# Sparse attention's compressed-branch values: two F32R passes on split operands in place of plain F32

## The chip, the cores and the metric

The kernel runs on one NeuronCore of a Trainium2 chip. The metric is device microseconds of one execution. The engines are named as in the profile: PE is TensorE (matmuls; PEld are its weight loads), DVE VectorE, ACT ScalarE, POOL GpSimd, SP the engine that issues the DMAs. PSUM is used as banks of 128 partitions by 512 words.

## The reference, cut to what matters

Two decoder layers over 512 positions of width 1024. Layer 0 has a gating MLP, differential attention and memory attention; layer 1 has a convolution module, a sparse attention with 8 heads in 2 groups, and memory attention. The change concerns one of three branches of the sparse attention: keys and values are compressed to 31 blocks, every query attends to the blocks that end before it, and the output of this branch is added, weighted by a gate, to those of the two others.

```python
kc = compress(k_cmp_raw, ...)              # 31 compressed keys a group
vc = compress(v_cmp_raw, ...)              # 31 compressed values a group, 64 wide
def block(args):                           # 128 queries
    s = einsum('bgrqd,bgnd->bgrqn', qi, kc) * scale
    p_c = masked_softmax(s, cmp_end <= qpos)
    o_c = einsum('bgrqn,bgnd->bgrqd', p_c, vc)
    ...                                    # o_s (selected blocks), o_w (window)
    return gt[..., 0:1] * o_c + gt[..., 1:2] * o_s + gt[..., 2:3] * o_w
```

## The kernel before

**Dense products.** A matrix is split in a high part, rounded to F32R, and a low part, the rest. A product is three F32R matmuls (high by high, high by low, low by high: L402, L403, L404 in `mm3`). The split of a weight is ACT's copy L386 and POOL's subtraction L389; the split of something in PSUM or of an activation is `split`: ACT's copy L376 and DVE's subtraction L377. Transposes are L399.

**Sparse attention** is `d_attn`, over query tiles in the order 3, 2, 1, 0 and two groups of four heads in each. `d_cattn` does the compressed branch of a tile for all 8 heads: scores L1148, softmax on DVE and ACT, transposes, and a copy (L1167) to `pc`, the weights of 32 compressed positions x 4 heads on the partitions, 128 queries along the free dimension, one such square a group. `d_cmp` has earlier put the compressed values in `cbd`: for head r of a group a block of 32 rows holds the 64 value columns, the other rows are zero, so that one product over 128 partitions picks out head r. L1184 does this product, plain F32, once a head, into rows 0 to 63 of the group's bank `o`.

The two other branches are steps (a, b) in the same loop: scores in L927, from PSUM with the mask by DVE's L929, exponentials in ACT's L1191, reciprocals and gates L1192 and L1193, a scaling on DVE (L576) or POOL (L574) in turn, transposes L399, a split to `pe`, and value products L1214: high and low part of the values side by side (128 weight columns, rows 0 to 127 of `o`), and the high part alone for the low part of `pe` (64 columns). A tile of index i has i + 1 key tiles; tiles 3 and 2 work on two heads a step, tiles 1 and 0 on four. After a group ACT copies the upper half of `o` (L1219), DVE adds it to the lower (L1220) and the gate multiplies (L582). There are two PSUM banks for scores, two for transposes and one for `o`.

**What runs beside it.** `merge` puts dense work between the steps: gate projections (`gates_T`, with DVE's L479), the end of the convolution (`c_finish`: DVE's L1305, L1307, L1309), then the output projection `out_part`, whose sums DVE adds to the residual (L657). The order in which the engines execute is fixed when the program is built: a scheduler lists instructions by priority and by when their operands and buffers are expected free.

**Pages.** Working tiles are pages of an arena. F32R tiles lie in arena "r", in pages of 2048 words a partition (kinds x and w), which `take` halves when half a page is enough; F32 tiles lie in arena "f". A page that was given back is taken again, and what is written to it must wait for the last reader. `take` goes by the smallest size with a free page, and prefers a larger one only while more than `RESERVE` (2 for x and w) of that size are free:

```python
sizes = [size for k, size in sorted(self.free) if k == kd and size >= words and self.free[k, size]]
if sizes:
    pick = sizes[0]
    for size in sizes[1:]:
        if words > 16 and size <= 4 * words and len(self.free[kd, size]) > RESERVE[kd in "xw"] \
                and self.free[kd, size][0][0] < self.free[kd, pick][0][0]:
            pick = size
```

While `d_attn` runs on tiles 3 and 2, two pages of kind x are free for it. A `pe` takes 1024 words (two key tiles) or 512.

Of the kernel before, what the change touches and what calls it, by code (L numbers as in the profile page):

```python
# [24 lines left out]
F32R = mybir.dt.float32r  # L25
BF16 = mybir.dt.bfloat16
AF = mybir.ActivationFunctionType
ALU = mybir.AluOpType
AX = mybir.AxisListType
ADD, SUB, MUL, MAX = ALU.add, ALU.subtract, ALU.mult, ALU.max  # L30

P = 128
# [253 lines left out]
def emit(ctx, tc, nc, D, out):  # L286
    sbp = ctx.enter_context(tc.tile_pool(name="sb", bufs=1))
# [4 lines left out]
              "p": Arena(psp.tile([P, words["p"]], F32, name="banks"), PAGES["p"])}  # L292
    cst_t = sbp.tile([P, CONST], F32, name="const")

    def SC():
        return Scope(arenas)
# [8 lines left out]
    V, A, G, mm = nc.vector, nc.scalar, nc.gpsimd, nc.tensor.matmul  # L305
    dma = nc.sync.dma_start
    act = A.activation
# [4 lines left out]
    def bc(ap, shape):  # L312
        return ap.broadcast_to(list(shape))
# [24 lines left out]
    def C(shape):  # L338
        n = int(np.prod(shape[1:]))
        v = cst_t[:shape[0], coff[0]:coff[0] + n]  # L340
        coff[0] += n
        assert coff[0] <= CONST
        if len(shape) == 3:
            v = v.rearrange("p (a b) -> p a b", a=shape[1])
        elif len(shape) == 4:
            v = v.rearrange("p (a b c) -> p a b c", a=shape[1], b=shape[2])
        return v
# [11 lines left out]
    def colp(n):  # L359
        o, l = COFF[n]  # L360
        return col[:, o:o + l]
# [6 lines left out]
    def rstd(sc, ss, scale, n, eps=EPS, parts=P):  # L368
        v = sc([P, n])[:parts]
        G.tensor_scalar(v, ss, scale, eps, MUL, ADD)  # L370
        r = sc([P, n])[:parts]
        G.tensor_tensor(r, v, mhalf[:parts, :n], ALU.pow)  # L372
        return r

    def split(src, h, l, eng=None):
        act(h, src, AF.Copy)  # L376
        (eng or V).tensor_tensor(l, src, f32(h), SUB)  # L377
# [20 lines left out]
    def tr(o, i, k=P):  # L398
        nc.tensor.transpose(o, i, ident[:k, :k])  # L399
# [27 lines left out]
    def proj_T(sc, hs, name, kind="d"):  # L427
        p = sc.ps(kind, [P, S])
        with SC() as wsc:
            (wh, wl), = load(wsc, name)  # L430
            wh = wh.rearrange("p (k c) -> p k c", k=KT)
            wl = wl.rearrange("p (k c) -> p k c", k=KT)
            for k in range(KT):
                mm3(p, wh[:, k, :], wl[:, k, :], hs[0][k // 4][:, k % 4, :], hs[1][k // 4][:, k % 4, :],
                    k == 0, k == KT - 1)
        return p
# [621 lines left out]


    ckt = sbp.tile([P, 2, 64], F32R, name="ckt")  # L1060
    cbd = C([P, 2, 4, 64])
    ccm = sbp.tile([P, NT, 32], BF16, name="ccm")

    def d_cmp():
        w2 = C([P, 2, 64])
        dma(w2, D["w2"].rearrange("p (a d) -> p a d", a=2))
        for j, nm in enumerate(("kc", "vc")):
            sc = SC()
            f = sc([P, 2, S])
            with SC() as pc:  # L1070
                p = proj_T(pc, h1, nm, "t")
                for g in range(2):
                    act(f[0:64, g, :], p[64 * g:64 * g + 64, :], AF.Copy)
                    V.tensor_copy(f[64:128, g, 0:511], p[64 * g:64 * g + 64, 1:512])
            yield UT
            w1 = [sc([P, 8, P], F32, k) for k in ("f", "raw")]
            for b in range(2):
                dma(w1[b], D["w1"][j, :, b * DM:(b + 1) * DM].rearrange("p (l c) -> p l c", l=8))
            fe = sc([P, 16, 64])
            f4 = fe.rearrange("p l (g j) -> p l g j", g=2)  # L1080
            pos = colp("posk" if j == 0 else "posv")
            G.memset(f4[:, :, :, 31:32], 0.0)
            for g in range(2):
                for a in range(2):
                    G.tensor_tensor(f4[:, 8 * a:8 * a + 8, g, 0:31],
                                    f[:, g, 16 * a:16 * a + 496].rearrange("p (j l b) -> p l j b", l=8, b=2)[:, :, :, 0],
                                    bc(pos[:, 8 * a:8 * a + 8].unsqueeze(2), [P, 8, 31]), ADD)
            hp = sc.ps("t", [64, P])
            for l in range(16):
                mm(hp, fe[:, l, :], w1[l // 8][:, l % 8, :], start=l == 0, stop=l == 15)  # L1090
            ht, th = sc([64, P]), sc([P, 64])
            act(ht, hp, AF.Tanh, scale=0.5)
            V.scalar_tensor_tensor(ht, ht, 1.0, hp, ADD, MUL)
            with SC() as pc:
                pt = pc.ps("t", [P, 64])
                tr(pt, ht, 64)
                V.tensor_copy(th, pt)
            o = sc.ps("t", [64, 64])
            mm(o, th, w2[:, j, :], start=True, stop=True)
            if j == 0:  # L1100
                t, u, d = sc([64, 64]), sc([64, 16]), sc([64, 2, 64])
                ss = sc([64, 1])
                act(t, o, AF.Square, accum_out=ss)
                r = rstd(sc, ss, 0.25 / 64, 1, parts=64)
                G.tensor_scalar(r, r, 0.5, None, MUL)
                V.tensor_tensor(t, o, ccg, MUL)
                V.tensor_tensor(u, o[:, 0:16], csg, MUL)
                V.tensor_tensor(t[:, 0:8], t[:, 0:8], u[:, 8:16], ADD)
                V.tensor_tensor(t[:, 8:16], t[:, 8:16], u[:, 0:8], ADD)
                V.tensor_scalar(d, bc(t.unsqueeze(1), [64, 2, 64]), r, None, MUL)  # L1110
                pt = sc.ps("d", [P, 64])
                tr(pt, d.rearrange("p a d -> p (a d)"), 64)
                split(pt.rearrange("p (g j) -> p g j", g=2), ckt[:, :, 0:32], ckt[:, :, 32:64])
            else:
                G.memset(cbd, 0.0)
                for g in range(2):
                    for r in range(4):
                        act(cbd[32 * r:32 * r + 32, g, r, :], o[32 * g:32 * g + 32, :], AF.Copy, scale=0.5)
            sc.close()
            yield 3700  # L1120
        G.memset(ccm, 0.0)
        G.affine_select(ccm, ccm, pattern=[[P, NT], [-16, 32]], compare_op=ALU.is_ge, fill=NEG, base=-31,
                        channel_multiplier=1)
        G.affine_select(ccm, ccm, pattern=[[0, NT], [-1, 32]], compare_op=ALU.is_ge, fill=NEG, base=30,
                        channel_multiplier=0)
# [17 lines left out]
    def d_cattn(i, pc):  # L1143

        with SC() as sc:
            s2 = sc.ps("s", [P, 8, 64])
            for h in range(8):
                mm(s2[:, h, :], dqs[i][0][:, h, :], ckt[:, h // 4], start=h == 0, stop=False)  # L1148
            mm(s2[:, :, 0:32], identb, bc(ccm[:, i:i + 1, :], [P, 8, 32]), start=False, stop=True)
            s = sc([P, 8, 32])  # L1150
            act(s, s2[:, :, 32:64], AF.Copy)
            V.tensor_tensor(s, s, s2[:, :, 0:32], ADD)
            mx, lc = sc([P, 8]), sc([P, 8])
            V.tensor_reduce(mx, s, AX.X, MAX)
            V.tensor_scalar(mx, mx, 0.1 * NEG, None, MAX)
            sm = sc([P, 8, 32])
            V.tensor_tensor(sm, s, bc(mx.unsqueeze(2), [P, 8, 32]), SUB)
            act(sm, sm, AF.Exp)
            V.tensor_reduce(lc, sm, AX.X, ADD)
            V.tensor_scalar(lc, lc, tiny, None, MAX)  # L1160
            V.reciprocal(lc, lc)
            V.tensor_tensor(lc, lc, dgt[:, i, :, 0], MUL)
            V.tensor_tensor(sm, sm, bc(lc.unsqueeze(2), [P, 8, 32]), MUL)
            pt = sc.ps("t", [P, 2, P])
            for g in range(2):
                tr(pt[:, g, :], sm[:, 4 * g:4 * g + 4, :].rearrange("p h j -> p (h j)"))
            act(pc, pt, AF.Copy)  # L1167
        yield CX

    def d_attn(yD, order, done):  # L1170

        for i in order:
            isc = SC()
            pc = isc([P, 2, P])
            yield from d_cattn(i, pc)
            for g in range(2):
                gsc = SC()
                o = gsc.ps("o", [P, 4, P])
                nh = 4 if i < WIDE else 2
                steps = [(a, b) for a in range(0, 4, nh) for b in range(2)]  # L1180
                for a, b in steps:
                    if (a, b) == steps[-1]:
                        for r in range(4):
                            mm(o[0:64, r, :], cbd[:, g, r, :], pc[:, g, :], start=False, stop=False)  # L1184
                    with SC() as sc:
                        es, nm = causal_scores(sc, i, [[(dqs[i][0][:, 4 * g + r, :], dkh[:, 2 * b + g, :]),
                                                        (dqs[i][0][:, 4 * g + r, :], dkl[:, 2 * b + g, :])]
# [9 lines left out]
                        for k0 in range(0, i + 1, kn):  # L1197
                            ks = range(k0, min(k0 + kn, i + 1))
                            n = len(ks)
                            with SC() as pc2:  # L1200
                                pt = pc2.ps("t", [P, n, nh, P])
# [5 lines left out]
                                for k in ks:  # L1207
# [5 lines left out]
                                    for m in ((hi, lo) if b + k == 0 else (lo, hi)):  # L1213
                                        mm(*m, start=m is hi and a + b + k == 0,  # L1214
                                           stop=m is hi and (a, b) == steps[-1] and k == i)
# [142 lines left out]
         "r": {"x": [(2048, 7)], "w": [(2048, 5)]},  # L1358
         "p": {"d": [(512, 6)], "t": [(512, 2)]}}
RESERVE = [3, 2]  # L1360
CONST = 3370

W_DENSE, W_ATTN, W_OUT, W_ATTN1 = 5, 5, 4, 2
P_DENSE, P_L0, P_MEM = (5, 0, 3, 0), (3, 2, 2, 1), (4, 2, 2, 0)
# [31 lines left out]
```

## Time and profile before

| | us |
|---|---|
| timed runs | 708.21, 708.18, 705.78 |
| their median | 708.18 |
| the profiled execution | 705.86 |
| its span | 704.1 |
| mean granted clock of PE | 0.99 |

The span runs from the first to the last instruction; the 1.76 us between it and the execution's time lie around it. A stretch's table gives each engine's busy time and, in brackets, its instructions; busy PE counts matmuls that overlap once, and the duration of one matmul (some 0.4 us for 512 columns) is longer than the distance to the next (0.23).

### The profile page before, as it was taken

How to read it: one execution, taken by the hardware profiler on the slowest of the kernel's cores; microseconds unless marked ns; L12 is line 12 of the kernel's file. 1: busy time of each engine (PE TensorE's matmuls, PEld its weight loads, DVE VectorE, ACT ScalarE, POOL GpSimd, SP SyncE). 2: the span in 40 equal slices, each digit the busy share in tenths (PEclk: the TensorE clock that was granted, in tenths of full speed). 3: DMA queues.
4: the chain of work that ended last, by engine and by line, in shares of the span. 5: the costliest groups of instructions: out<-in, count | busy, mean ns of one | idle time of the engine just before them, and what ended most of it. 6: DMA issues, size and time to landing. Idle time of an engine off the chain costs nothing.

```text
span 704.1 us, 11050 instructions
## 1 busy us (share of the span) xinstructions
PE 667.0 (95%) x3819; PEld 564.9 (80%) x3819; DVE 496.6 (71%) x1204; ACT 376.8 (54%) x846; POOL 392.7 (56%) x414
## 2 busy tenths in 40 slices
PE   4999989999999979989989999898999999999997
PEld 3789989888888867878878888776777888788875
DVE  4606678667666975763474968998867776998773
ACT  6345346556455772762453568642346666676541
POOL 3467887575336763255854789965564523421650
PEclk9999999999999988999999999999999999999999
DMA  8532135564313352123332421104121101120121
GB/s 316 174 119 91 61 90 152 142 169 131 105 53 121 104 174 82 61 91 110 105 102 80 150 76 48 57 1 150 36 85 60 61 31 60 54 68 1 61 76 74
DMA packets 22376, 66.56 MB, mean 95 GB/s; under 512 B 3504, under 2 KB 3760, under 8 KB 22320
## 3 DMA queue, kind: packets, MB, share of 16 engines
q1 hardware_dynamic: 22320, 65.86, 28.7%
q8 instruction: 30, 0.49, 0.3%
q14 instruction: 26, 0.21, 0.1%
HBM read 57.46 MB, written 2.10 MB: 85 GB/s over the span
## 4 chain that ended last, share of the span: by engine, by line
PE 72%; DVE 12%; POOL 6%; ACT 4%; issue 3%; DMA 3%; SPq 0%; ACTq 0%; POOLq 0%; DVEq 0%
PE banks L403 18%; PE banks L402 18%; PE banks L404 18%; PE banks L399 6%; PE banks L927 4%; DVE arena_r L377 3%; POOL arena_r L389 3%; DMA arena_f<-in_wall_dram 2%; POOL arena_f L372 2%; PE banks L1214 2%; PE banks L965 2%; ACT arena_r L386 1%; DVE arena_f L929 1%; PE banks L1090 1%; PE banks L1184 1%
## 5 line engine op out<-in xcount | busy, mean ns | idle before, releaser
L389 POOL TENSOR_TENSOR arena_r<-arena_f,arena_r 128x512 fp32r<-128x512 f32 (+1 forms) x174 | 228.6, 1339 | 174.9 <-ACT arena_r L386 171.1
L402 PE MATMUL banks<-arena_r 128*128 128x512 f32 (+2 forms) x784 | 289.7, 374 | 5.6 <-ACT arena_r L386 2.3
L403 PE MATMUL banks<-arena_r 128*128 128x512 f32 (+2 forms) x784 | 290.3, 371 | 2.4 <-POOL arena_r L389 1.4
L404 PE MATMUL banks<-arena_r 128*128 128x512 f32 (+2 forms) x784 | 288.8, 370 | 1.5 <-DVE arena_r L377 1.5
L402 PEld LDWEIGHTS banks<-arena_r 128*128 128x128 f32 x784 | 148.6, 190 | 31.2 <-ACT arena_r L386 3.7
L403 PEld LDWEIGHTS banks<-arena_r 128*128 128x128 f32 x784 | 149.0, 190 | 26.1 <-POOL arena_r L389 2.9
L404 PEld LDWEIGHTS banks<-arena_r 128*128 128x128 f32 x784 | 148.8, 190 | 24.2 <-DVE arena_r L377 2.2
L386 ACT ACTIVATE arena_r<-arena_f 128x1024 fp32r<-128x1024 f32 (+2 forms) x87 | 91.1, 1049 | 74.2 <-DMA arena_f<-in_wall_dram 19.8
L399 PE MATMUL banks<-const,arena_f 128*128 128x128 f32 x507 | 83.4, 281 | 15.8 <-DVE arena_f L417 8.9
L377 DVE TENSOR_TENSOR arena_r<-banks,arena_r 128x512 fp32r<-128x512 f32 (+1 forms) x112 | 67.1, 608 | 27.6 <-ACT arena_r L376 27.1
L376 ACT ACTIVATE arena_r<-banks 128x512 fp32r<-128x512 f32 (+1 forms) x112 | 57.7, 532 | 51.6 <-PE banks L399 36.5
L399 PEld LDWEIGHTS banks<-const,arena_f 128*128 128x128 f32 x507 | 62.4, 145 | 28.3 <-DVE arena_f L417 9.3
L929 DVE CUSTOM_DVE_ANT_0 arena_f<-banks,const 128x512 f32<-128x512 f32 (+3 forms) x128 | 60.5, 485 | 32.4 <-PE banks L927 26.8
L372 POOL TENSOR_TENSOR arena_f<-arena_f,const 128x4 f32<-128x4 f32 (+3 forms) x60 | 68.0, 1136 | 3.6
L1263 DVE SCALAR_TENSOR_TENSOR banks<-arena_f,const,banks 128x482 f32<-128x482 f32 (+14 forms) x90 | 66.1, 734 | 1.3
L927 PE MATMUL banks<-arena_r 128*128 128x512 f32 (+7 forms) x192 | 50.8, 338 | 4.4 <-DVE arena_f L929 2.1
L1191 ACT ACTIVATE arena_f<-arena_f 128x256 f32<-128x256 f32 (+3 forms) x64 | 35.7, 559 | 25.9 <-DVE arena_f L929 25.1
L958 ACT ACTIVATE arena_f<-arena_f 128x512 f32<-128x512 f32 (+3 forms) x64 | 35.7, 561 | 25.0 <-DVE arena_f L929 24.4
L657 DVE TENSOR_TENSOR arena_f<-arena_f,banks 128x512 f32<-128x512 f32 x40 | 27.0, 684 | 25.4 <-PE banks L404 24.6
L574 POOL TENSOR_SCALAR arena_f<-arena_f 128x512 f32<-128x512 f32 (+3 forms) x32 | 19.9, 626 | 39.6 <-DVE arena_f L1193 33.7
L927 PEld LDWEIGHTS banks<-arena_r 128*128 128x128 f32 (+1 forms) x192 | 32.8, 190 | 10.6 <-DVE arena_f L929 4.7
L1261 POOL TENSOR_TENSOR arena_f<-arena_f 128x482 f32<-128x482 f32 (+29 forms) x30 | 37.8, 1258 | 2.3 <-ACT arena_f L1260 0.6
(177 smaller groups left out, 811.6 us busy)
## 6 DMA issues: line engine op xcount, KB each, us to landing
arena_f<-in_wall_dram SPq DMA_DIRECT2D x88, 512.0 KB, 3.3
arena_r<-arena_r SPq DMA_DIRECT2D x96, 64.0 KB, 2.0
arena_f<-in_x_dram SPq DMA_DIRECT2D x7, 512.0 KB, 4.7
arena_f<-in_w_dram SPq DMA_DIRECT2D x4, 512.0 KB, 3.8
out_dram<-arena_f SPq DMA_DIRECT2D x8, 256.0 KB, 2.0
arena_f<-in_norms_dram SPq DMA_DIRECT2D x3, 512.0 KB, 4.2
arena_f<-in_mem_dram SPq DMA_DIRECT2D x2, 512.0 KB, 3.3
arena_f<-in_wqb_dram SPq DMA_DIRECT2D x2, 420.0 KB, 3.2
```

Of the source, the lines that this page charges most:

```text
L372: G.tensor_tensor(r, v, mhalf[:parts, :n], ALU.pow)
L376: act(h, src, AF.Copy)
L377: (eng or V).tensor_tensor(l, src, f32(h), SUB)
L386: act(h, raw, AF.Copy)
L389: G.tensor_tensor(l[:, c], raw[:, c], f32(h[:, c]), SUB)
L399: nc.tensor.transpose(o, i, ident[:k, :k])
L402: mm(o, lh, rh, start=first, stop=False)
L403: mm(o, lh, rl, start=False, stop=False)
L404: mm(o, ll, rh, start=False, stop=last)
L927: mm(t[:, a % per, :], q, k[:, :w], start=b == 0, stop=b == len(qk) - 1)
L929: V.tensor_tensor_reduce(e[a], t[:, a % per, :], cmask[:, S - w:], -1.0, -NEG, ADD, ALU.min, nm[:, a:a + 1])
L1263: V.scalar_tensor_tensor(acc[:, z:], hc[:, :S - z], cw[:, f, k:k + 1], acc[:, z:], MUL, ADD)
```

## The change

`pc` becomes a split pair (two squares a group, F32R), written by `split` instead of a copy. `cbd` becomes an F32R tile of its own with the high and the low part of the values side by side; the compressed values are scaled and split once (`cs`), and eight copies of 128 columns put both parts in their places. Each product becomes two: both parts of the values by the high part of the weights into all 128 rows of `o`, and the high part of the values by the low part of the weights into rows 0 to 63. `pc` has 512 words for 256, and moves from arena f to arena r, for as long as its tile lasts.

```diff
-    cbd = C([P, 2, 4, 64])
+    cbd = sbp.tile([P, 2, 4, 2, 64], F32R, name="cbd")
...
-                G.memset(cbd, 0.0)
+                G.memset(f32(cbd), 0.0)
+                cs = sc([64, 2, 64], F32R)
+                act(cs[:, 0, :], o, AF.Copy, scale=0.5)
+                V.scalar_tensor_tensor(cs[:, 1, :], o, 0.5, f32(cs[:, 0, :]), MUL, SUB)
                 for g in range(2):
                     for r in range(4):
-                        act(cbd[32 * r:32 * r + 32, g, r, :], o[32 * g:32 * g + 32, :], AF.Copy, scale=0.5)
+                        act(cbd[32 * r:32 * r + 32, g, r], f32(cs[32 * g:32 * g + 32]), AF.Copy)
...
-            act(pc, pt, AF.Copy)
+            split(pt, pc[:, 0], pc[:, 1])
...
-            pc = isc([P, 2, P])
+            pc = isc([P, 2, 2, P], F32R)
...
-                            mm(o[0:64, r, :], cbd[:, g, r, :], pc[:, g, :], start=False, stop=False)
+                            mm(o[:, r, :], cbd[:, g, r].rearrange("p a d -> p (a d)"), pc[:, 0, g, :], start=False,
+                               stop=False)
+                            mm(o[0:64, r, :], cbd[:, g, r, 0, :], pc[:, 1, g, :], start=False, stop=False)
...
-CONST = 3370
+CONST = 2858
```

The scheduler's order changes with it, on all engines from the start of `d_attn` on. Below are three places on PE. In the changed kernel L1214, the value products, are L1219, and L1184 is the pair L1187 and L1189; lines up to 1060 keep their numbers. "128x512" is the output's partitions and columns, "x4" a count.

Tile 3, before: four value products of a split, the transposes of the next, the next tile's compressed scores, and the next value products.

```order
L1214 MATMUL banks<-arena_r 64x256
L1214 MATMUL banks<-arena_r 128x256
L1214 MATMUL banks<-arena_r 64x256
L1214 MATMUL banks<-arena_r 128x256
L399 MATMUL banks<-const,arena_f 128x128 x4
L1148 MATMUL banks<-ckt,arena_r 128x64 x8
L1149 LDWEIGHTS identb
L1149 MATMUL banks<-ccm,identb 128x8x32
L1214 MATMUL banks<-arena_r 64x256
L1214 MATMUL banks<-arena_r 128x256
```

Tile 3, changed, one of the gaps: the transposes that follow four value products, and the first value product of the next split.

```order
L399 MATMUL banks<-const,arena_f 128x128 x4
L404 MATMUL banks<-arena_r 128x512
L402 MATMUL banks<-arena_r 128x512
L403 MATMUL banks<-arena_r 128x512
L404 MATMUL banks<-arena_r 128x512
L402 MATMUL banks<-arena_r 128x512
L403 MATMUL banks<-arena_r 128x512
L404 MATMUL banks<-arena_r 128x512
L402 MATMUL banks<-arena_r 128x512
L403 MATMUL banks<-arena_r 128x512
L404 MATMUL banks<-arena_r 128x512
L1219 MATMUL banks<-arena_r 128x256
```

Ten dense matmuls stand between them.

Tile 2, before: value products and transposes, and the dense matmuls behind them (those shown and eight more).

```order
L1214 MATMUL banks<-arena_r 64x256
L1214 MATMUL banks<-arena_r 128x256
L1214 MATMUL banks<-arena_r 64x256
L1214 MATMUL banks<-arena_r 128x256
L399 MATMUL banks<-const,arena_f 128x128 x2
L1214 MATMUL banks<-arena_r 64x256
L1214 MATMUL banks<-arena_r 128x256
L399 MATMUL banks<-const,arena_f 128x128 x4
L404 MATMUL banks<-arena_r 128x512
L402 MATMUL banks<-arena_r 128x512
L403 MATMUL banks<-arena_r 128x512
L404 MATMUL banks<-arena_r 128x512
```

Tile 2, changed: value products, transposes and scores.

```order
L1219 MATMUL banks<-arena_r 128x256
L1219 MATMUL banks<-arena_r 64x256 x2
L1219 MATMUL banks<-arena_r 128x256
L1219 MATMUL banks<-arena_r 64x256
L1219 MATMUL banks<-arena_r 128x256
L399 MATMUL banks<-const,arena_f 128x128 x4
L927 MATMUL banks<-arena_r 128x384 x2
L1219 MATMUL banks<-arena_r 64x256
L1219 MATMUL banks<-arena_r 128x256
L1219 MATMUL banks<-arena_r 64x256
L1219 MATMUL banks<-arena_r 128x256
L399 MATMUL banks<-const,arena_f 128x128 x2
```

No dense matmul stands among these twelve rows; there are 6 in the whole stretch from tile 3's last compressed products to tile 2's, where there were 87.

The end of the program, before: tile 0's compressed products, the last two value products, and the first of the 24 dense matmuls behind them.

```order
L1184 MATMUL banks<-arena_f,const 64x128 x4
L1214 MATMUL banks<-arena_r 64x512
L1214 MATMUL banks<-arena_r 128x512
L402 MATMUL banks<-arena_r 128x512
L403 MATMUL banks<-arena_r 128x512
L402 MATMUL banks<-arena_r 128x512
L403 MATMUL banks<-arena_r 128x512
L404 MATMUL banks<-arena_r 128x512
L402 MATMUL banks<-arena_r 128x512
L403 MATMUL banks<-arena_r 128x512
L404 MATMUL banks<-arena_r 128x512 x2
```

The end, changed: the last two value products and the first of the 18 dense matmuls behind them.

```order
L1219 MATMUL banks<-arena_r 64x512
L1219 MATMUL banks<-arena_r 128x512
L402 MATMUL banks<-arena_r 128x512
L403 MATMUL banks<-arena_r 128x512
L404 MATMUL banks<-arena_r 128x512
L402 MATMUL banks<-arena_r 128x512
L403 MATMUL banks<-arena_r 128x512
L404 MATMUL banks<-arena_r 128x512
L402 MATMUL banks<-arena_r 128x512
L403 MATMUL banks<-arena_r 128x512
L402 MATMUL banks<-arena_r 128x512
L403 MATMUL banks<-arena_r 128x512
```

In both, the last twelve dense matmuls are those that need the last group's output; before, twelve others stand ahead of them, and in the changed kernel six.

## Rows read from the trace of the kernel before

**Rows 1.** The page: the span, and each engine's busy time, share and instructions.

```profile
span 704.1 us, 11050 instructions
...
PE 667.0 (95%) x3819; PEld 564.9 (80%) x3819; DVE 496.6 (71%) x1204; ACT 376.8 (54%) x846; POOL 392.7 (56%) x414
```

**Rows 2.** Stretches: from:to, length, then PE, PEld, DVE, ACT, POOL busy; clock; DMA.

```profile
527.63:564.98 37.35, 37.24 (x199) 30.00 (x198) 27.87 (x77) 23.50 (x58) 17.51 (x17) 1.00 0.18 57
564.98:588.81 23.83, 23.83 (x148) 21.00 (x147) 18.04 (x54) 13.80 (x31) 7.96 (x8) 1.00 0.13 45
588.81:633.48 44.67, 43.20 (x266) 37.12 (x265) 40.48 (x110) 32.74 (x80) 16.67 (x15) 1.00 0.18 60
633.48:693.82 60.34, 58.84 (x320) 47.52 (x319) 46.16 (x132) 30.48 (x81) 23.21 (x28) 1.00 0.14 49
693.82:704.10 10.28, 6.47 (x27) 4.67 (x26) 3.32 (x6) 1.01 (x2) 0.00 (x0) 1.00 0.20 77
595.37:638.48 43.11, 41.65 (x255) 35.52 (x255) 39.76 (x110) 29.10 (x74) 16.11 (x17) 1.00 0.18 62
```

**Rows 3.** The chain that ended last: start us, us, what; two stretches of it.

```profile
589.46 0.70 PE banks L927 x4
...
637.11 0.47 PE banks L927 x4
...
655.95 0.40 PE banks L927 x4
...
692.88 1.02 PE banks L1184 x8
...
317.95 0.23 PE banks L403
...
319.75 0.06 PE banks L586
```

**Rows 4.** POOL at the start, then by line and form: the split's subtraction, the copies.

```profile
1.79 0.53 POOL L1115 MEMSET const<- 128x512 f32 x1
...
5.17 0.19 POOL L414 TENSOR_TENSOR arena_f<-arena_f 128x1 f32<-128x1 f32 x1 [1.67 <-ACT arena_f L412]
...
L377 DVE TENSOR_TENSOR arena_r<-banks,arena_r 128x256 fp32r<-128x256 f32 x8 | 3.3, 411 | 0.0
...
L1118 ACT ACTIVATE const<-banks 32x64 f32<-32x64 f32 x8 | 1.7, 212 | 0.1
```

**Rows 5.** By line and form, 520 to 704 us: DVE's groups, xcount | busy us, mean ns.

```profile
L657 DVE TENSOR_TENSOR arena_f<-arena_f,banks 128x512 f32<-128x512 f32 x24 | 16.1, 683 | 8.0 <-PE banks L404 7.8
...
L929 DVE CUSTOM_DVE_ANT_0 arena_f<-banks,const 128x384 f32<-128x384 f32 x16 | 8.7, 550 | 2.8 <-PE banks L927 2.4 <-PE banks L399 0.4
...
L479 DVE SCALAR_TENSOR_TENSOR arena_f<-arena_f,banks 128x512 f32<-128x512 f32 x8 | 5.5, 683 | 1.2 <-ACT arena_f L478 1.1
...
L576 DVE TENSOR_SCALAR arena_f<-arena_f 128x256 f32<-128x256 f32 x8 | 4.9, 658 | 0.1
...
L1307 DVE SCALAR_TENSOR_TENSOR arena_f<-arena_f 128x512 f32<-128x512 f32 x4 | 3.8, 951 | 0.1
...
L1309 DVE SCALAR_TENSOR_TENSOR arena_f<-arena_f,const 128x512 f32<-128x512 f32 x4 | 3.0, 760 | 0.0
...
L1305 DVE TENSOR_TENSOR arena_f<-arena_f 128x512 f32<-128x512 f32 x4 | 2.5, 684 | 0.0
```

**Rows 6.** In order of time, the last value products and what follows them.

```profile
693.82 0.68 PE L1214 MATMUL banks<-arena_r 128*64 128x512 f32 x2
...
694.54 0.59 ACT L1219 ACTIVATE arena_f<-banks 64x512 f32<-64x512 f32 x1 [1.44 <-PE banks L1214]
...
695.88 0.85 DVE L582 SCALAR_TENSOR_TENSOR arena_f<-arena_f 64x256 f32<-64x256 f32 x2
...
696.76 0.42 ACT L376 ACTIVATE arena_r<-arena_f 128x256 fp32r<-128x256 f32 x1 [1.63 <-DVE arena_f L582]
...
697.23 0.50 PE L402 MATMUL banks<-arena_r 128*128 128x512 f32 x1
```

**Rows 7.** Stretches of 5 us in layer 0; the clock is third from the end.

```profile
255.00:260.00 5.00, 2.84 (x15) 2.17 (x13) 4.76 (x8) 4.48 (x12) 5.00 (x5) 1.00 0.59 210
260.00:265.00 5.00, 4.04 (x16) 3.05 (x16) 4.75 (x20) 3.49 (x14) 2.71 (x4) 0.53 0.63 204
305.00:310.00 5.00, 3.14 (x23) 2.32 (x22) 4.96 (x8) 4.06 (x13) 5.00 (x5) 1.00 0.44 124
```

## The prediction

> **What bounds the kernel now.** First the page: the tensor engine (PE) is busy 95% of a span of 704.1 us, the vector engine 71%, and no other engine is near [rows 1]. That is an average, so the next view is the table of stretches over layer 1's sparse attention, the only place where the change acts. I cut it at the four tensor-engine moments at which the compressed branch's products end for a query tile (tile 3 ends at 588.81, tile 2 at 633.48, tile 0 at 693.82). Column 3 is PE, column 5 DVE. Up to 588.81 PE has no gap to speak of: 37.24 of 37.35 and 23.83 of 23.83 us. In tile 2's stretch PE is still busy 43.20 of 44.67, but DVE 40.48: both are nearly full. The last row is the same stretch between two marks of DVE's own (the addition L1220 of tile 3's and tile 2's second head group): 39.76 busy of 43.11, or 92% [rows 2]. So before the change PE sets the time almost everywhere, and DVE would set it in tile 2's stretch if PE had less to do there. Those two readings carry the forecast.
>
> **The products themselves.** The chain of waits gives the price of a matmul where PE sets the pace. Plain F32 runs as two instructions: L1184's group of four products is 8 instructions and 1.02 us, so 0.255 us a product [rows 3]. There are 4 tiles x 2 groups x 4 heads = 32. Now each product is two F32R passes over 128 columns, one with 128 weight columns, one with 64. Both shapes are in the trace: four score products of 128 columns on 128 weight columns (L927) take 0.40, 0.10 each, and the memory attention's value products, 64 weight columns and 128 moving ones, 0.06 each [rows 3]. So 0.16 instead of 0.255: 32 x 0.095 = 3.0 us less on PE. Bounds: 2 x 0.06 would save 4.3; a pass of each kind at the old half-price of 0.1275 saves nothing. I take 3.0, since both rows have the shape wanted.
>
> The Trainium skill ("TensorE: Matmul & The Clock Gate", Back-to-back issue gap) puts an isolated matmul of 128 columns at about 56 ns whatever its weights. By it the pair would cost 0.11 and the saving be 4.6; the 0.10 of the 128-weight row speaks against it, and its section LDWEIGHTS, which charges by weight columns, explains why.
>
> **The operand work.** Tile by tile, the copy L1167 becomes a split: one more DVE subtraction of 128x256 from a bank, 0.41 [rows 4], four in all, 1.6 us, in a stretch where DVE has room except for tile 1's, which falls into tile 2's stretch. The eight copies L1118 of 0.21 read 128 instead of 64 columns, plus a scaled copy and a subtraction of 64x64: under 1 us on ACT, which is busy 23.50 of 37.35 there; cost nothing, at most that 1 us. The memset at 1.79 doubles from 0.53 on POOL, and POOL then stands idle 1.67 waiting for ACT before its next work [rows 4]: nothing.
>
> **What the order does.** This is the larger part. The weights pc now live in the arena of F32R pages, and take a quarter of one of the two 2048-word pages that the split exponentials pe used in turn. `take` prefers the smallest page that fits, and that is now the 1024-word remainder; the whole second page stays unused, because a larger size is only chosen while more than two of it are free. So through tile 3 consecutive pe share one place, and a split must wait until the value products L1214 of the one before have read it. The order shows the answer: ten to fourteen dense matmuls stand between one group of value products and the next, where there were none at the same place. Counting dense matmuls (L402 to L404) between the marks: tile 3 gets 210 where it had 135, tile 2 gets 6 where it had 87, tiles 1 and 0 get 150 for 156, and behind the last compressed products stand 36 for 24. None is lost; 402 both times.
>
> Tile 3: PE was full and is full. Its longer stretch costs nothing by itself; it is work brought forward.
>
> Tile 2: between DVE's marks PE loses 81 dense at 0.23 = 18.6, ten scores of 384 columns at 0.175 and four of 256 at 0.117 = 2.2, and 0.76 on eight products: 21.6 [rows 3]. It would need 43.1 - 21.6 = 21.5 us. DVE loses, between the same marks, four L1305 (2.5), four L1307 (3.8), three of four L1309 (2.25), two of eight L479 (1.4), two of 24 L657 (1.3), three scalings L576 of some 0.6 (1.8) and one subtraction (0.4), and gains one L929 of 0.5 [rows 4, 5]: 13.0, so 26.8 us remain. DVE now needs more than PE: PE waits 26.8 - 21.5 = 5.2 us if DVE runs without a gap, and 7.5 if it stays at 92% (29.0). At the other end, nothing, if what DVE doesn't finish slides into the next stretch, where it was busy 46.16 of 60.34 [rows 2]. I take 5.2: the two score banks let PE run only a pair of heads ahead of DVE, so it can't slide far, and the nearest row is the 92% one.
>
> The end: after the last value products (693.82) a chain runs over ACT (694.54), DVE (695.88) and ACT (696.76), and the products that need it start at 697.23 [rows 6]. Twelve dense matmuls, 2.75 us, cover it now. In the new order six of the covering ones have gone ahead of it, so six are left: 6 x 0.23 = 1.4 us of wait. Bounds 0 and 2.
>
> **Sum.** -3.0 + 5.2 + 1.4 = +3.6 us. The profiled execution took 705.86, so it would be 709.5. It is at the low end of the three timed runs; their median is 708.18, and from that the forecast is 711.8. What this measurement can tell from no change is about 0.5%, 3.5 us: up to 704.6 is faster, from 711.7 slower.
>
> **Rivals.**
> *The wait is hidden (0.25).* PE has so much work ready that DVE's surplus slides on; then -3.0 and at most the 1.4 of the end: 705 to 706.6. For it: PE waited only 1.47 us in tile 2's stretch although DVE was 91% busy [rows 2]. Against: it had 87 dense matmuls there to bridge gaps, and has 6.
> *One page for pe sets the pace (0.15).* In tile 2 the order puts only four transposes and two scores, some 0.8 us, between value products where the ACT copy and the DVE subtraction need about 1.3. Eight splits of 1024 words by 0.5 to 0.7 add 4 to 5.5 on top if they don't coincide with DVE's own queue: 716 to 717. It decides once ACT's L376 waits for value products in most splits there.
> *The clock falls in the thin stretch (0.05).* The granted clock went to 0.53, the lower level of 1.2 GHz, at 260 to 265 after PE had been busy 2.84 of 5 us; but at 305 to 310 it kept 1.00 with 3.14 of 5 [rows 7]. Tile 2's stretch would have 21.5 of 26.8. Five to ten us at half clock add 2.5 to 5 of PE work, part of it behind DVE: 713 to 716.
> The Trainium skill ("TensorE: Matmul & The Clock Gate", HAM oscillation) blames idle gaps between bursts for such falls; the waits here are many and short, which by it keeps the clock up.
> *The passes save nothing (0.05)*, both at the old half-price: 714.8.
>
> **Chances.** The forecast itself has 0.5, with a range of its own from 708.5 to 715.5, half of it past the 711.7. With the page, the clock and the empty passes, slower gets 0.46. The hidden wait and the lower half of the forecast make 0.40 for the same; 0.14 for faster is the hidden wait with the 4.3 of the lower bound, or an order that happens to close waits I can't see. Eight in ten: 704 to 717.
>
> **What would show it.** Right: L1187 and L1189 together near 0.16 a product; PE busy under 85% between the ends of tile 3's and tile 2's compressed products, DVE over 92% there, the longest waits of PE for L377, L576 and L929; tile 3 some 19 us longer; over 1 us of PE idle before the last twelve products. Wrong: PE as full in tile 2 as before, or the stretch shorter than 25 us; or ACT's L376 waiting for value products there, which is the second rival.

## The result: 1.5% slower, and the profile after

The changed kernel took 718.01 us (median of four runs, 717.49 to 719.03), the kernel before 708.19 beside it. The ratio is 1.0149, with a 95% interval from 1.0124 to 1.0173: some 10.5 us slower. The profiled executions differ by 717.49 - 705.86 = 11.6 us, and their spans by as much.

The page of the changed kernel first, to lay beside [rows 1]: PE's busy time went up by 2.3 us although its products got cheaper, and its share went down.

```profile
span 715.7 us, 11050 instructions
...
PE 669.3 (94%) x3819; PEld 565.0 (79%) x3819; DVE 497.4 (69%) x1209; ACT 378.5 (53%) x847; POOL 392.4 (55%) x414
```

Next the stretches, cut at the same marks as [rows 2] and with the same columns (length, PE, PEld, DVE, ACT, POOL, clock, DMA). The first two together are tile 3, then come tile 2, tiles 1 and 0, and the end.

```profile
528.54:583.67 55.13, 51.55 (x264) 40.61 (x264) 37.76 (x103) 30.54 (x72) 23.11 (x22) 1.00 0.17 58
583.67:616.89 33.22, 32.13 (x179) 26.25 (x178) 21.40 (x49) 18.01 (x35) 14.23 (x12) 1.00 0.15 48
616.89:645.76 28.87, 22.54 (x162) 18.49 (x160) 28.32 (x87) 21.30 (x60) 3.76 (x6) 1.00 0.11 37
645.76:700.98 55.22, 54.71 (x316) 46.37 (x315) 44.03 (x137) 31.05 (x85) 22.89 (x28) 1.00 0.14 49
700.98:715.70 14.72, 9.86 (x44) 7.11 (x42) 4.69 (x8) 1.61 (x3) 0.00 (x0) 0.96 0.19 71
```

Against [rows 2]: the start of the attention is 0.9 later, tile 3 takes 88.35 instead of 61.18 (+27.2), tile 2 28.87 instead of 44.67 (-15.8), tiles 1 and 0 55.22 instead of 60.34 (-5.1), the end 14.72 instead of 10.28 (+4.4). The sum is 11.6, the whole difference.

How much of tile 3 is work? It holds 75 dense matmuls more (75 x 0.23 = 17.3 us), ten of tile 2's score products (10 x 0.175 = 1.8) and eight small products of the convolution that stood in tile 2 before (L1302, 1.2 in the chain below), and its own compressed products are some 0.7 cheaper. That makes 19.6 of the 27.2 and leaves some 8 us that no added work explains. They are seen on PE: it was idle for 0.11 us there before, and for 55.13 - 51.55 + 33.22 - 32.13 = 4.67 now; the rest lies in matmuls that count as busy but follow each other more slowly. The waits of tile 3 (engine, line, whom it waits for: us in total, times, longest), after and then before:

```profile
ACT arena_r L376 <- PE banks L1219: 11.7, 5, 3.7
DVE arena_f L929 <- PE banks L399: 10.2, 4, 3.9
...
PEld banks L927 <- DVE arena_f L929: 5.3, 7, 2.8
```

```profile
ACT arena_r L376 <- PE banks L1214: 5.3, 2, 2.9
...
PEld banks L927 <- DVE arena_f L929: 0.5, 2, 0.3
```

ACT's half of the split (L376) waits for the value products twice as long, and the score products (L927) now wait for DVE's reading of the score banks (L929), which in its turn stood 10.2 us for PE. A piece of the changed kernel's timeline shows how the first of these arises (start, duration, engine, line; in brackets the wait before it):

```profile
609.47 0.39 PE L403 MATMUL banks<-arena_r 128*128 128x512 f32 x1
609.70 0.65 PE L1219 MATMUL banks<-arena_r 128*64 128x256 f32 x4
...
610.18 0.60 PE L399 MATMUL banks<-const,arena_f 128*128 128x128 f32 x4
610.44 0.60 ACT L376 ACTIVATE arena_r<-banks 128x512 fp32r<-128x512 f32 x1 [1.85 <-PE banks L1219]
...
611.08 0.69 DVE L377 TENSOR_TENSOR arena_r<-banks,arena_r 128x512 fp32r<-128x512 f32 x1 [0.19 <-ACT arena_r L376]
```

The four value products stand on PE behind twelve dense matmuls in a row. Until they have read the one page, the next split may not write it, so ACT stands for 1.85 us with a split that needs nothing else, and whatever is queued behind it on ACT stands too. The dense matmuls were put there to fill the wait for the page; they also lengthen it.

The products themselves: one pair, from the chain of waits (start us, us, what), and ahead of it the eight small products of the convolution.

```profile
588.67 1.16 PE banks L1302 x8
...
616.43 0.11 PE banks L1187
616.55 0.06 PE banks L1189
```

### The profile page after: what moved, and what is told of

Read it like the earlier page. It is cut to its first block, busy times and chain, and to the rows that moved or that the text cites. A ratio compares the mean times of both kernels' runs of the same rounds, so it can differ in the third digit from the quotient of the medians.

```text
span 715.7 us, 11050 instructions
## 1 busy us (share of the span) xinstructions
PE 669.3 (94%) x3819; PEld 565.0 (79%) x3819; DVE 497.4 (69%) x1209; ACT 378.5 (53%) x847; POOL 392.4 (55%) x414
## 4 chain that ended last, share of the span: by engine, by line
PE 69%; DVE 14%; POOL 6%; ACT 5%; issue 3%; DMA 3%; SPq 0%; ACTq 0%; POOLq 0%; DVEq 0%
PE banks L404 18%; PE banks L402 18%; PE banks L403 18%; PE banks L399 5%; DVE arena_r L377 4%; POOL arena_r L389 3%; PE banks L927 3%; DMA arena_f<-in_wall_dram 2%; POOL arena_f L372 2%; PE banks L965 2%; DVE arena_f L929 2%; PE banks L1219 2%; ACT arena_r L386 1%; PE banks L1090 1%; ACT arena_r L376 1%
## 5 line engine op out<-in xcount | busy, mean ns | idle before, releaser
L389 POOL TENSOR_TENSOR arena_r<-arena_f,arena_r 128x512 fp32r<-128x512 f32 (+1 forms) x174 | 228.7, 1339 | 173.0 <-ACT arena_r L386 162.7
L399 PE MATMUL banks<-const,arena_f 128*128 128x128 f32 x507 | 84.9, 284 | 17.1 <-DVE arena_f L417 9.8
L376 ACT ACTIVATE arena_r<-banks 128x512 fp32r<-128x512 f32 (+1 forms) x116 | 60.1, 527 | 70.7 <-PE banks L399 45.0
L377 DVE TENSOR_TENSOR arena_r<-banks,arena_r 128x512 fp32r<-128x512 f32 (+1 forms) x116 | 69.1, 602 | 34.1 <-ACT arena_r L376 33.4
L929 DVE CUSTOM_DVE_ANT_0 arena_f<-banks,const 128x512 f32<-128x512 f32 (+3 forms) x128 | 60.5, 483 | 39.1 <-PE banks L927 23.3
L399 PEld LDWEIGHTS banks<-const,arena_f 128*128 128x128 f32 x507 | 63.2, 147 | 29.1 <-DVE arena_f L417 10.2
L927 PE MATMUL banks<-arena_r 128*128 128x256 f32 (+7 forms) x192 | 52.3, 340 | 8.3 <-DVE arena_f L929 6.1
L927 PEld LDWEIGHTS banks<-arena_r 128*128 128x128 f32 (+1 forms) x192 | 33.0, 190 | 15.6 <-DVE arena_f L929 9.8
```

The costliest lines, as they stand in the source:

```text
L389: G.tensor_tensor(l[:, c], raw[:, c], f32(h[:, c]), SUB)
L927: mm(t[:, a % per, :], q, k[:, :w], start=b == 0, stop=b == len(qk) - 1)
L929: V.tensor_tensor_reduce(e[a], t[:, a % per, :], cmask[:, S - w:], -1.0, -NEG, ADD, ALU.min, nm[:, a:a + 1])
```

## The experiments

"Tile 3" means in all of them the stretch from where tile 3's first eight compressed score products are through to the end of its compressed products; the window rows have the columns of [rows 2].

**A page of its own for the weights.** The changed kernel, with one F32R page of 512 words that only `pc` uses; the exponentials keep both their pages.

```
- "r": {"x": [(2048, 7)], "w": [(2048, 5)]},
+ "r": {"x": [(2048, 7)], "w": [(2048, 5)], "q": [(512, 1)]},
- pc = isc([P, 2, 2, P], F32R)
+ pc = isc([P, 2, 2, P], F32R, "q")
```

> The changed kernel, but pc lies in a 512-word F32R page of its own kind, so that the two 2048-word pages are free for pe as before the change. The order puts 48, 48, 36, 12, 25, 47, 56 and 40 dense matmuls behind the marks, near the 50, 49, 38, 14, 23, 81, 38, 24 of before. Theory page (the shared place of pe and the order it forces cost the time): the products save 3 us and nothing else is lost, 704 to 708 on a kernel before of 708. Rival operands (the split, the second pass and the larger copies cost more than they save, wherever pc lies): 713 or more. Rival any-order (the scheduler's order is a matter of luck, and any new one is worse): 712 or more.

Measured: 706.51 us, ratio 0.9993 (0.9976 to 1.001). By the ratios, 11.0 us of the changed kernel's loss go when the page is its own, and what is left of the change, cheaper products and operand work, moves the time by -0.5, which the interval doesn't tell from nothing. The range for the page held, but the 3 us that the products were to save don't show in the time. The stretches, tile 3 to the end:

```profile
528.05:591.00 62.95, 62.41 (x356) 52.02 (x356) 47.66 (x140) 41.06 (x96) 26.15 (x26) 1.00 0.15 51
591.00:633.63 42.63, 40.00 (x256) 35.13 (x255) 39.04 (x108) 29.61 (x74) 15.40 (x16) 1.00 0.19 63
633.63:688.22 54.59, 52.52 (x302) 44.23 (x300) 42.46 (x128) 29.64 (x80) 21.81 (x26) 1.00 0.13 44
688.22:703.90 15.68, 10.48 (x48) 7.93 (x46) 5.57 (x10) 1.61 (x3) 0.00 (x0) 1.00 0.22 84
```

PE is busy 165.42 us over these rows (169.6 over the first five of [rows 2]), so 4.2 us of PE's work are gone. But it is idle 10.4 instead of 6.9: 2.6 instead of 1.5 in tile 2, 2.1 instead of 1.5 in tiles 1 and 0, 5.2 instead of 3.8 at the end. What PE saved it waits. (The products account for some 3 of the 4.2; the rest no run explains.)

**The page without the products.** The kernel before, holding an unwritten F32R page of 512 words through every tile, and a second version that holds it in tile 3 alone.

```
  pc = isc([P, 2, P])
+ isc([P, 512], F32R)          # second version: only if i == 3
```

> The kernel before, with its plain F32 products, but a 512-word F32R page that nobody writes is held for as long as pc. Dense matmuls behind the marks: 96, 6, 6, 36, 48, 56, 28, 12. Theory page: the loss of the changed kernel without its saving, 10 + 3 = 13 us more than before, 718 to 723. Rival operands: 708, since no operand changes.

> The kernel before with the unwritten 512-word page held during tile 3 only. Dense matmuls behind the marks: 96, 6, 6, 12, 38, 47, 47, 36. If the page costs mainly in tile 3 (its splits wait for the value products, and the dense work is used up there): nearly all of what the page costs in all tiles, 10 us or more. If it costs in every tile alike: a third of it, 4 us.

Measured: 726.04 us, ratio 1.0253 (1.0222 to 1.0285), and with tile 3 alone 720.72, ratio 1.0182 (1.0155 to 1.0209). The page alone, with the old products and the old copy, costs 17.9 us, and 12.9 when it is held in tile 3 alone. The second is as expected; the first lies above its range of 718 to 723. In its profiled execution the granted clock was 0.98 in tile 3, 0.95 in tile 2 and 0.73 at the end, where the changed kernel had 1.00, 1.00 and 0.96, so part of the excess is clock. Tile 3 of the two:

```profile
530.29:619.04 88.75, 85.06 (x437) 68.21 (x436) 58.94 (x147) 47.03 (x104) 38.14 (x35) 0.98 0.16 54
```

```profile
529.07:617.73 88.66, 84.93 (x438) 68.19 (x437) 58.96 (x147) 47.04 (x104) 38.16 (x35) 0.98 0.17 54
```

Both have the changed kernel's 88.35 within 0.4 us, and 210 dense matmuls there like it (though at a clock of 0.98 for its 1.00, so the lengths are not alike in every part). The second kernel's tile 2 is thin too (29.70 us) though no page is held in it: it is thin because tile 3 took its work.

**Both pages back in turn, without more memory.** The changed kernel with the reserve of `take` set to 0 ahead of the attention, so that the second 2048-word page is chosen.

```
+ RESERVE[1] = 0
  drain(merge((ahead(d_attn(yD, rev, done), HD), 1.0),
```

> The changed kernel, but from the start of the sparse attention take may choose a larger page that was freed earlier however few there are (RESERVE 0 for F32R pages), so that pe uses the 1024-word rest and the other 2048-word page in turn, while pc stays where it is. Dense matmuls behind the marks: 48, 65, 7, 8, 35, 53, 60, 36. It parts the two costs: if the wait of consecutive splits in tile 3 is the larger one, tile 3 (from 527.6 to its second compressed products) comes back to within 2 us of its PE work and the run to 708 to 712; if the thin stretch of tile 2 is, it stays near 714 or more, since tile 2 still has only 15 dense matmuls.

Measured: 710.55 us, ratio 1.0041 (1.0023 to 1.006). Tile 3 is back at 62.94 us, the own-page version's length. But this doesn't part the wait from a thin tile 2, as was meant: the order has 65 + 7 = 72 dense matmuls in tile 2's stretch, and the 15 of the expectation were read between the wrong marks. Both went back to near what they were. What still separates the two is PE's busy time, 168.43 us over the attention for 165.42 (idle 10.9 and 10.4): another order, and in tile 2 a clock of 0.92. Tiles 3 and 2:

```profile
527.89:590.83 62.94, 62.39 (x356) 52.03 (x356) 47.69 (x140) 41.07 (x96) 26.16 (x26) 1.00 0.16 51
590.83:633.15 42.32, 38.88 (x235) 34.18 (x234) 37.65 (x97) 27.72 (x67) 15.02 (x14) 0.92 0.19 63
```

**The wait or the crowd?** In the changed kernel two things differ in tile 3 at once: one page instead of two, and 210 dense matmuls instead of 135. Two kernels pull them apart. The own-page version with a planner's number that puts 210 there as well, and the changed kernel with a share that puts fewer there.

```
- CD, CX = 80, 3600                                        (own-page version)
+ CD, CX = 80, 30000
...
- drain(merge((ahead(d_attn(yD, rev, done), HD), 1.0),     (changed kernel)
+ drain(merge((ahead(d_attn(yD, rev, done), HD), 1.2),
```

> The own-page version with CX at 30000 instead of 3600, nothing left out. The planner then puts as many dense matmuls into tile 3 as the changed kernel has there (210, the own-page version 138), but the split exponentials still have two pages in turn. What counts is the length from the first compressed score product to the end of tile 3's compressed products (own-page version 62.95 us, changed kernel 88.35). Theory 'the wait for the one page cost the 8.6 us that the work brought forward doesn't explain': 62.95 + 72 x 0.233 = 79.7, between 78.5 and 81.5. Rival 'so many dense matmuls between the attention steps hold up its chains whatever the pages': 86 to 90. The whole time is no test here; with so little dense work left for the later tiles it will be over the own-page version's, 710 to 725.

> The changed kernel, with the attention's share in the planner's merge at 1.2 instead of 1.0, nothing left out: the split exponentials share one page in tile 3 as in the changed kernel, but only 162 dense matmuls stand there instead of 210. Length of tile 3, as above: theory 'the wait for the page': 62.95 + 24 x 0.233 = 68.5 for the work, and on top the whole 8.6 or more, since there is less to cover the waits: 77 to 82. Rival 'the dense matmuls hold up the chains': 8.6 x 24/72 = 2.9 on top, 69 to 72. The whole time is no test.

Measured: 724.04 and 727.53 us in all, no test, as said. Tile 3 took 81.00 us with two pages and 210 dense matmuls, and 75.56 with one page. First row the first kernel's, then the second's:

```profile
530.09:611.09 81.00, 78.34 (x422) 64.01 (x422) 53.35 (x135) 45.84 (x96) 31.55 (x28) 1.00 0.18 59
```

```profile
535.12:610.68 75.56, 70.81 (x374) 57.30 (x374) 52.54 (x145) 44.94 (x104) 34.03 (x33) 0.95 0.15 50
```

The first lies in the range of the wait, but its stretch also lost 12 of tile 2's score products (2.1 us) that the range had counted in. The second falls between the two ranges, and 18 of the 162 dense matmuls turned out to stand ahead of the mark: the trace has 144 in the stretch. So both are counted again from the own-page version's 62.95, with 0.23 for a dense matmul, 0.175 for a score of 384 columns and 1.2 for the eight products L1302, which all three kernels have there and the own-page version has not:

- The changed kernel has 72 dense and 4 scores more, 81.4 us of work. Some 7 us are unexplained.
- The first kernel has 72 dense more and 12 scores fewer, 78.6 (two smaller products fewer take off some 0.4). Some 3 are unexplained, with two pages.
- The second has 6 dense and 8 scores more, 66.9 (less some 0.5 likewise). Some 9 are unexplained, but the granted clock fell there:

```profile
600.00:608.00 8.00, 7.14 (x32) 6.47 (x32) 4.59 (x14) 2.80 (x7) 1.33 (x2) 0.57 0.06 26
```

7.14 us of busy PE at 0.57 would be some 4 at 1.00 (an estimate), so some 3 of the 9 are clock, and 6 are left. So in the changed kernel the page brings some 4 of the 7 us, the larger part; up to 3 come with the crowd of dense matmuls whatever the pages. That the page costs more where less fills the wait isn't shown. ACT's split waited longer for the value products with one page; first the changed kernel's thin version, then the crowded one with two pages:

```profile
ACT arena_r L376 <- PE banks L1219: 13.0, 5, 5.8
```

```profile
ACT arena_r L376 <- PE banks L1219: 7.6, 4, 3.8
```

**Can the saved 4 us be had?** Three kernels with one planner's number changed, so that the dense matmuls stand elsewhere: the own-page version with CX or with FILLG, and the kernel before with the same CX.

```
- CD, CX = 80, 3600
+ CD, CX = 80, 4500                  (own-page version; control: the kernel before)
...
- FILLG, FILLC, GLU1 = 0.8, 0.12, 1
+ FILLG, FILLC, GLU1 = 1.0, 0.12, 1  (own-page version)
```

> The own-page version with one number of the planner changed (CX, the planned cost of a tile's compressed scores, 4500 instead of 3600), nothing left out. It spreads the dense matmuls otherwise: 48, 50, 34, 24, 32, 62, 38 and 24 after the eight groups of compressed products, where the own-page version had 48, 48, 36, 12, 25, 47, 56 and 40, and the kernel before 50, 49, 38, 14, 23, 81, 38 and 24. Theory 'the two passes do save 3 to 4 us, and the own-page version lost them again where its order left the tensor engine idle' (3.8 us idle at the end grew to 5.2, some 2 us more in tile 2's second half, 2 us in tile 1): with 24 again behind the last products and 24 instead of 12 in tile 2's second half it takes 702 to 705 us where the kernel before takes about 706.6, a ratio of 0.993 to 0.998. Rival 'what the passes save, the operand work takes': the same as before whatever the order, a ratio of 0.999 to 1.001.

> Control: the kernel before, with plain F32 products, and CX at 4500. Dense matmuls after the eight groups: 47, 50, 42, 24, 32, 83, 19 and 22. If the version with own page and CX is faster only because CX is better, this one is faster than before by as much (ratio 0.993 to 0.998). Theory 'the passes give it': within 1.5 us of before, a ratio of 0.998 to 1.003, since before had only 1.2 us of idle in tile 2's second half to win back.

> The own-page version with another number of the planner changed (FILLG, 1.0 instead of 0.8), nothing left out: 48, 48, 36, 14, 22, 67, 53 and 24 dense matmuls after the eight groups. Tile 2's second half stays as thin as in the own-page version (14 for 12), the end has the 24 of before. Theory as for the version with CX: only the 1.4 us of the end come back, 704.5 to 706 us, a ratio of 0.997 to 0.999. Rival: 0.999 to 1.001.

Measured: with CX 713.79 us, ratio 1.0085 (1.0061 to 1.0109); the control 715.56, ratio 1.0113 (1.0089 to 1.0136); with FILLG 709.35, ratio 1.003 (1.001 to 1.005). All three expectations failed. Counting dense matmuls behind the last products doesn't forecast the end: the CX version has 24 there, as the kernel before, and its end is 14.96 us long. (With FILLG the 24 did bring the end back, to 10.18 us, but tile 2 took 46.54 at a clock of 0.96 for the own-page version's 42.63 at 1.00, with 84 dense matmuls in both.) The CX version's PE, in order of time:

```profile
701.78 0.62 PE L1219 MATMUL banks<-arena_r 128*64 128x512 f32 x2
705.13 0.50 PE L402 MATMUL banks<-arena_r 128*128 128x512 f32 x1 [2.73 <-ACT arena_r L376]
705.47 0.39 PE L403 MATMUL banks<-arena_r 128*128 128x512 f32 x1
...
706.98 0.63 PE L403 MATMUL banks<-arena_r 128*128 128x512 f32 x1
```

Only the twelve dense matmuls that need the last group's output were left behind the last value products, so PE waited the whole chain, and then the clock fell, to near the lower level of 1.2 GHz in the next stretch, where dense matmuls follow each other at 0.43 instead of 0.23 us:

```profile
701.00:704.00 3.00, 1.40 (x7) 0.76 (x5) 0.90 (x3) 0.59 (x1) 0.00 (x0) 1.00 0.00 0
...
707.00:710.00 3.00, 2.74 (x7) 1.64 (x5) 0.91 (x2) 0.00 (x0) 0.00 (x0) 0.57 0.12 47
```

The Trainium skill ("TensorE: Matmul & The Clock Gate", HAM oscillation) blames idle gaps for such falls; this trace agrees in so far as one of 2.73 us stands just ahead of the fall.

What the pair does tell is the price of the products in a second order. The stretches from tile 1 to the end, own-page version and control:

```profile
636.18:698.64 62.46, 57.85 (x319) 48.04 (x317) 47.43 (x132) 29.35 (x80) 22.25 (x26) 0.97 0.13 47
698.64:713.60 14.96, 8.37 (x32) 5.86 (x30) 4.01 (x7) 1.61 (x3) 0.00 (x0) 0.87 0.14 53
```

```profile
636.43:700.73 64.30, 60.84 (x321) 49.05 (x320) 46.91 (x131) 30.15 (x82) 21.57 (x26) 0.97 0.13 46
700.73:714.00 13.27, 6.73 (x29) 4.60 (x28) 4.01 (x7) 1.61 (x3) 0.00 (x0) 0.95 0.15 58
```

Over the whole attention PE is busy 168.91 us in the first and 172.22 in the control, idle 15.13 and 12.63. So once more 3.3 us of work go, 2.5 come back as waiting, and 0.8 are left, as between the own-page version and the kernel before (4.2, 3.5 and 0.6). These are two single executions; the medians of this pair lie 1.8 us apart, with intervals that overlap. By these rows the operand work isn't what takes the gain; PE's waits are. No version here beats the kernel before by what can be told from no change.

## Why the prediction was wrong

The direction was right, the size was not: +3.6 us forecast, +10.5 measured, 1 us past the range.

- **The products: right in price.** The pair costs 0.11 + 0.06, forecast 0.16. By the isolated 56 ns of the Trainium skill ("TensorE: Matmul & The Clock Gate", Back-to-back issue gap) it would have cost 0.11. The section itself says that this figure leaves out the loading of weights, and the measured 0.17 agrees that it is too low here. But the 3 us were booked as time. In the own-page version the time moved by 0.5, within its interval of nothing.
- **Tile 3: the step that failed.** "Tile 3: PE was full and is full. Its longer stretch costs nothing by itself; it is work brought forward." It was to be some 19 us longer and is 27 longer. PE isn't full there any more (idle for 4.67 us, 0.11 before), and some 8 us, a term that the sum put at nothing, are no work. With two pages the stretch takes 62.95 us at 138 dense matmuls and 81.00 at 210; with one page 88.35 at 210. The sum had the right cause in its hand, "a split must wait until the value products L1214 of the one before have read it", and priced it at nothing, since dense matmuls stood in the gaps. They filled PE, but ACT, DVE and the score banks behind the split waited. With both pages back, in its own page or by the reserve, the 8 us are gone.
- **Tile 2: right.** The 26.8 us were forecast between DVE's marks (the additions of the second head groups, 43.11 before), with 21.5 for PE. Between the same marks the changed kernel has 26.14, PE busy 21.45:

```profile
622.93:649.07 26.14, 21.45 (x158) 18.40 (x158) 25.79 (x92) 19.88 (x60) 4.61 (x7) 1.00 0.07 21
```

Between PE's marks it is 28.87, with PE busy 78% and DVE 98% (foreseen: under 85% and over 92%). That PE's figure is so near is in part luck: its sum left out the convolution's eight products that moved away, some 1 us. The changed kernel's longest waits of PE there are for L377, as foreseen:

```profile
PE banks L1219 <- DVE arena_r L377: 4.6, 5, 1.4
ACT arena_r L376 <- PE banks L1219: 4.3, 6, 1.4
...
PE banks L927 <- DVE arena_f L929: 0.9, 2, 0.6
```

- **The end: right.** PE was to wait 1.4 us more; it is idle 4.86 instead of 3.81, and the clock fell to 0.96. The changed kernel's chain is that of [rows 6], later:

```profile
705.54 0.63 PE L1219 MATMUL banks<-arena_r 128*64 128x512 f32 x2
...
706.20 0.59 ACT L1224 ACTIVATE arena_f<-banks 64x512 f32<-64x512 f32 x1 [2.55 <-PE banks L1219]
...
708.43 0.42 ACT L376 ACTIVATE arena_r<-arena_f 128x256 fp32r<-128x256 f32 x1 [1.63 <-DVE arena_f L582]
...
708.89 0.50 PE L402 MATMUL banks<-arena_r 128*128 128x512 f32 x1 [0.76 <-ACT arena_r L376]
```

- **The rivals.** The page as the pacemaker was the right mechanism in the wrong tile. It was looked for in tile 2, where ACT's split did wait for value products, in 6 of 18 splits out of PSUM and 4.3 us in all, but where the length came out as forecast without it. It decided in tile 3, where the order showed one page in use and the sum put nothing. The falling clock didn't happen in the changed kernel's tile 2 (1.00 at PE busy 22.54 of 28.87). It did in the same thin stretch of the kernel that holds the page in tile 3 alone, where PE's waits were many and none was over 1.1 us:

```profile
621.00:624.00 3.00, 1.47 (x9) 1.00 (x9) 3.00 (x9) 2.64 (x8) 0.53 (x1) 0.89 0.00 0
624.00:627.00 3.00, 3.00 (x13) 3.00 (x14) 3.00 (x10) 1.69 (x6) 0.00 (x0) 0.54 0.01 3
```

So the prediction's sentence that many short waits keep the clock up isn't borne out here. The hidden wait and the empty passes are refuted by tile 2's row and by the price of the pair.
- **Left open.** How the 8 us of tile 3 split between wait and crowd is estimated (some 3 for the crowd), not settled: the two kernels that pull them apart differ in score products, in clock and in where the dense ones stand. And PE's longest wait in the changed kernel's tile 3, 2.40 of its 4.67 idle us, comes behind slow DVE operations (last section) and isn't shown to be the page's. An order kept word for word with the page alone changed wasn't tried, since the planner follows the pages.

## What to carry to other kernels

When an operand changes its type, ask which pool of buffers it now draws from and who used that pool in turn: a quarter of a page taken from a double buffer cost 11 us here, where all the rest of the change moved the time by 0.5. Filling the wait for a buffer with other work of the same engine keeps that engine busy and can make everybody behind the buffer wait longer, so such a stretch is to be priced by its chain and not by its busy share. And work saved on an engine that is 95% busy is time only where that engine was what ended last; in two orders here some 3 to 4 us saved gave 0.5 to 2, none of it clear of the noise.

## What the runs showed that was not expected

A tiny DVE operation can take as long as a large one while POOL's subtraction L389 runs. In the changed kernel's tile 3 the 128x2 product L1198 has a median of 162 ns over its twelve, but took 1208 at its worst; the scaling after it was slow too, and the score products waited for DVE for 2.40 us:

```profile
555.60 2.51 POOL L389 TENSOR_TENSOR arena_r<-arena_f,arena_r 128x512 fp32r<-128x512 f32 x2 [5.93 <-ACT arena_r L386]
...
555.69 1.21 DVE L1198 TENSOR_TENSOR arena_f<-arena_f,const 128x2 f32<-128x2 f32 x1
...
556.93 1.45 DVE L576 TENSOR_SCALAR arena_f<-arena_f 128x512 f32<-128x512 f32 x1
...
559.05 0.73 PE L927 MATMUL banks<-arena_r 128*128 128x512 f32 x2 [2.40 <-DVE arena_f L929]
```

No run changed POOL's work, but the traces speak for it. The same product (L1193 before) stands 16 times in each of nine of the kernels, and takes 139 to 166 ns wherever no POOL operation runs at its start. Nineteen times it started while an L389 ran, and in 18 of these it ended 15 to 21 ns after that L389, whether 189 ns or 1259 had gone by; the last time, with 61 ns of L389 left, it took its usual 149.

And one number of the planner moves the time by nearly as much as the change did: CX at 4500 instead of 3600 costs 8 us with the old products and 6.5 with the new on their own page, by the order alone.
